# A first norm by plain transposes: raw x^T kept and used again as the residual

## Chip, cores and metric

The kernel runs on one core of a Trainium2 chip. The metric is the device time of one execution in microseconds, median over the runs. PE is the matrix engine, PEld its weight loads, DVE the vector engine, ACT the scalar (activation) engine, POOL the GpSimd engine, SP the engine whose queue issues most transfers.

## The reference, cut to what matters

One layer of a hybrid decoder for 1024 prompt tokens and 8 single-token samples, 1032 tokens in all, model width 1024. What the change touches:

```
def rmsnorm(x, w):
    y = x * rsqrt(mean(x * x, axis=-1, keepdims=True) + EPS)
    return y * w

def decoder_layer(x, ...):
    h = rmsnorm(x, norm1_w)
    q_r, f_r, i_r, g_r, z, xbc_r, dt_r = split(h @ w_in)    # w_in has 6672 columns, the last 16 are dt
    ...                                                     # HGRN2 heads, Mamba-2 mixer
    dt = softplus(dt_r + ssm_dt_bias);  A = -exp(ssm_a_log)
    ...
    x = x + concatenate([o_a, y]) @ w_out                   # the residual
    h = rmsnorm(x, norm2_w)
    ...                                                     # gated MLP with a convolution, second residual
```

All arrays are fp32. A final RMSNorm follows.

## The kernel before

Activations are held transposed: features on the 128 partitions, tokens along the row. The 1032 tokens are cut into three chunks of 344 (`CH`, `chunks`), the model width into eight column tiles of 128 (`KT`). Each fp32 operand of a large product is split in a high part that PE reads at its fast fp32r rate and a low remainder; a product is three matmuls: high times high, low times high, high times low (`prod`, `steps`).

First stage (`first_norm`, L106 to L130, and the loop at L402 to L405). Token tiles of x (128 tokens by 1024, `xt`) are loaded by SP. For three tiles at a time ACT squares them in two halves and sums (L115), DVE and ACT form 1/rms (L116 to L118), and DVE scales an identity by it (`dg`, L119). For each column tile PE multiplies the x tile by `dg` (L127, recorded at L93, the line of the helper `mm`), which transposes and normalises in one step into a PSUM bank (`tp`, four banks). ACT writes the high part `hT_hi` times the norm weight (L128), DVE the low part `hT_lo` (L129). After each group the first two column tiles of the state projection (`first`, tiles 8 and 10, which are B and C of group 0) are multiplied for one chunk of tokens and evicted by `xbc_evict`. A planner orders the instructions of all engines in this stage by its own costs; only PE is written in a fixed order later (`tc.manual_schedule`).

Behind the stage stand the convolution states (`conv_state`, which loads rows `rt` into the shared row buffers of tag "s", eleven of them, and transposes them), the closing of tiles 8 and 10 (`xbc_close`: convolution on DVE, SiLU on ACT), and the dt projection (L426 to L438): its weight is split in high and low halves side by side in 32 columns (`wdt`), and 48 matmuls, 16 a chunk, give `dtr`. Then come the softplus as a chain of short DVE operations (L464 to L480), Exp of `ssm_a_log` (L482), the cumulative sums, and the next column tiles, each with a weight loaded by `wload` (high part cast by ACT at L188, low part by DVE at L189, two buffers each).

The residual is added far later. The output projection runs as jobs `o8.m`, `o12.m`, `o0.m`, `o4.m`. The jobs `o8.m` open the sums: ACT copies the product out of PSUM (L1076), and x is loaded again from its input (`residual_load`, pieces of 128 by 512 with short rows), transposed by PE (L801, L805, tiles `xtp` and `xtd`), and added by DVE (L796). The generator `residual` is spread over the products that follow.

Of the kernel before, what the change touches and what calls it, by code (L numbers as in the profile page):

```python
# [16 lines left out]
P = 128  # L17
# [33 lines left out]
def hybrid_layer(  # L51
# [54 lines left out]
    def first_norm(tiles, then=()):  # L106

        xs = []
        for i in tiles:
            xt, t0, n = xtm[i]  # L110
            sq = half("xn")
            ss = keep.tile([P, 4], F32, tag="ss", bufs=4, name=nm("ss"))
            dg = tl("z", "dg")[:, :P]
            for i in range(2):
                A.activation(sq[:n], xt[:n, i * 512:(i + 1) * 512], AF.Square, accum_out=ss[:n, i:i + 1])  # L115
            V.tensor_tensor(ss[:n, 2:3], ss[:n, 0:1], ss[:n, 1:2], op=ALU.add)  # L116
            A.activation(ss[:n, 3:4], ss[:n, 2:3], AF.Sqrt, bias=epsc[:n], scale=1.0 / DM)
            V.reciprocal(ss[:n, 3:4], ss[:n, 3:4])  # L118
            V.tensor_scalar(dg[:n, :n], ident[:n, :n], ss[:n, 3:4], None, op0=ALU.mult)  # L119
            xs.append((xt, dg, t0, n))  # L120
        for work_ in then:
            work_()
        c0, c1 = xs[0][2], xs[-1][2] + xs[-1][3]
        for k in range(KT):
            tp = bank("tp")
            for xt, dg, t0, n in xs:
                mm(tp[:, t0 - c0:t0 - c0 + n], xt[:n, k * P:(k + 1) * P], dg[:n, :n])  # L127
            A.activation(hT_hi[k][:, c0:c1], tp[:, :c1 - c0], AF.Copy, scale=col("n1", k))  # L128
            V.scalar_tensor_tensor(hT_lo[k][:, c0:c1], tp[:, :c1 - c0], col("n1", k),  # L129
                                   hT_hi[k][:, c0:c1].bitcast(F32), op0=ALU.mult, op1=ALU.subtract)  # L130

# [28 lines left out]
    make_identity(nc, ident)  # L160
    epsc = keep.tile([P, 1], F32, name="epsc")
# [18 lines left out]
    def wload(src, kt, m=P, then=None):  # L180
# [6 lines left out]
        def rounded():  # L187
            A.copy(wh[:, :n], ws[:, :n])  # L188
            V.tensor_tensor(wl[:, :n], ws[:, :n], wh[:, :n].bitcast(F32), op=ALU.subtract)  # L189

        if then is None:
            rounded()
        else:
            then.append(rounded)
# [202 lines left out]
    rounded = []  # L397
    first = [(j, wload(w_in_[0, :, OFF_X + j * P:OFF_X + (j + 1) * P], KT, then=rounded), xbc_open()) for j in (8, 10)]
    for i in range(3, 9):
        load_x(i)  # L400
# [1094 lines left out]
```

## Time and profile before

| | |
|---|---|
| median of 3 runs | 1801.93 us (1798.46 to 1803.37) |
| span of the profiled execution | 1794.6 us (the page gives no other time for it) |
| PE busy | 1741.0 us, 97% |
| DVE, ACT, POOL busy | 1116.6, 789.1, 409.8 us |
| first matmul of the stage, first product | 9.77 us, 15.49 us |
| end of the third chunk's products | 54.33 us |
| end of the dt products | 63.50 us |
| residual transposes | 850 to 939 us |

A row of a timeline reads: start, length, engine, line, operation, output tile and inputs, count in a merged row, and in brackets the idle time before and what ended it. A matmul of two fp32 operands that aren't fp32r is counted as two PE instructions; a transpose as one. Matmuls overlap in the pipeline, so starts, not lengths, give their cost.

### The profile page before, as it was taken

The numbers are of one execution on the slowest core, as the hardware profiler recorded it, in microseconds if no ns is written. First come the engines' busy times: TensorE is split into PE (matmuls) and PEld (weight loads), VectorE is DVE, ScalarE is ACT, GpSimd is POOL, SyncE is SP. The second block draws the span as 40 slices with busy tenths as digits, with TensorE's granted clock in tenths as the row PEclk, the third lists the DMA queues.
The fourth block names the chain that finished last, engine by engine and source line by source line (L and its number), as shares of the span: only waits on it lengthen the run. The fifth ranks groups of instructions, "written<-read, shape, count | busy, mean of one in ns | idle before, by whom it ended". The sixth has DMA issues, their size and how long they took to land.

```text
span 1794.6 us, 38584 instructions
## 1 busy us (share of the span) xinstructions
PE 1741.0 (97%) x16215; PEld 1685.0 (94%) x16215; DVE 1116.6 (62%) x2002; ACT 789.1 (44%) x1414; POOL 409.8 (23%) x415
## 2 busy tenths in 40 slices
PE   7999899999999999999999988999999999999998
PEld 7998798999999999999999978999999999999997
DVE  4658967556555564557746769666666667555545
ACT  6477688454544444345323344333433334111114
POOL 1103331110110110110100364455444542000001
PEclk9999999999999999999999998999999999999999
DMA  5135634553222221235334431222222225422212
GB/s 154 36 98 155 171 100 138 175 147 99 72 77 63 78 79 50 74 96 159 94 107 130 133 116 48 94 73 71 75 85 90 72 71 193 150 95 96 96 60 95
DMA packets 218018, 182.34 MB, mean 102 GB/s; under 512 B 13388, under 2 KB 195158, under 8 KB 217830
## 3 DMA queue, kind: packets, MB, share of 16 engines
q1 hardware_dynamic: 217558, 179.80, 32.5%
q8 instruction: 127, 2.08, 0.5%
q14 instruction: 45, 0.37, 0.1%
q0 software_dynamic: 288, 0.10, 0.0%
HBM read 141.53 MB, written 38.52 MB: 100 GB/s over the span
## 4 chain that ended last, share of the span: by engine, by line
PE 77%; DVE 8%; ACT 6%; DMA 5%; issue 2%; POOL 2%; SPq 0%; DVEq 0%; POOLq 0%; ACTq 0%
PE mm L93 30%; PE ub L93 14%; PE dn L93 13%; PE ua L93 10%; PE a L93 2%; PE o L93 1%; DMA csb<-cs_d 1%; ACT csb L549 1%; PE tp L93 1%; DVE wl L189 1%; DMA Bb<-bc_d 1%; PE kv L93 1%; DMA Sd<-in_state_ssm_dram 1%; DMA out_dram<-Sd 1%; DVE xbc L352 1%
## 5 line engine op out<-in xcount | busy, mean ns | idle before, releaser
L93 PE MATMUL mm<-hh,wh 128*128 128x344 f32 x1248 | 406.2, 326 | 2.6 <-ACT sz L685 2.6
L93 PE MATMUL mm<-hl,wh 128*128 128x344 f32 x1248 | 403.9, 324 | 0.0
L93 PE MATMUL mm<-hh,wl 128*128 128x344 f32 x1248 | 402.8, 323 | 0.0
L93 PEld LDWEIGHTS mm<-hh,wh 128*128 128x128 f32 x1248 | 234.6, 188 | 5.9 <-ACT sz L685 2.9
L93 PEld LDWEIGHTS mm<-hh,wl 128*128 128x128 f32 x1248 | 234.9, 188 | 2.4 <-issue 1.2
L93 PEld LDWEIGHTS mm<-hl,wh 128*128 128x128 f32 x1248 | 234.6, 188 | 2.5 <-issue 0.9
L188 ACT CAST wh<-ws 128x1024 fp32r<-128x1024 f32 x96 | 100.6, 1048 | 265.4 <-PE dn L93 135.8
L93 PE MATMUL ub<-ul,wh 128*128 128x258 f32 x704 | 199.6, 284 | 4.2 <-DVE ul L1182 4.2
L93 PE MATMUL ub<-uh,wh 128*128 128x258 f32 x704 | 201.1, 286 | 2.0 <-ACT uh L1181 2.0
L93 PE MATMUL ub<-uh,wl 128*128 128x258 f32 x704 | 200.8, 285 | 0.0
L93 PE MATMUL dn<-ah,wh 128*128 128x256 f32 (+1 forms) x640 | 180.7, 282 | 1.2 <-DVE x L1425 1.2
L93 PE MATMUL dn<-al,wh 128*128 128x256 f32 (+1 forms) x640 | 180.3, 282 | 0.0
L93 PE MATMUL dn<-ah,wl 128*128 128x256 f32 (+1 forms) x640 | 179.9, 281 | 0.0
L93 PE MATMUL mm<-mh,wh 128*128 128x258 f32 x512 | 148.2, 290 | 10.7 <-DVE x L1078 8.1
L189 DVE TENSOR_TENSOR wl<-ws,wh 128x1024 fp32r<-128x1024 f32 x96 | 125.3, 1306 | 52.5 <-ACT wh L188 52.3
L93 PE MATMUL ua<-ul,wh 128*128 128x258 f32 x528 | 148.9, 282 | 0.9 <-DVE ul L1182 0.9
L93 PE MATMUL ua<-uh,wl 128*128 128x258 f32 x528 | 149.4, 283 | 0.0
L93 PE MATMUL ua<-uh,wh 128*128 128x258 f32 x528 | 149.2, 282 | 0.0
L93 PE MATMUL mm<-ml,wh 128*128 128x258 f32 x512 | 146.5, 286 | 0.0
L93 PE MATMUL mm<-mh,wl 128*128 128x258 f32 x512 | 146.1, 285 | 0.0
L93 PEld LDWEIGHTS ub<-ul,wh 128*128 128x128 f32 x704 | 134.6, 191 | 4.9 <-DVE ul L1182 4.9
L93 PEld LDWEIGHTS ub<-uh,wh 128*128 128x128 f32 x704 | 134.2, 191 | 2.5 <-ACT uh L1181 2.5
(331 smaller groups left out, 3925.0 us busy)
## 6 DMA issues: line engine op xcount, KB each, us to landing
ws<-in_w_in_dram SPq DMA_DIRECT2D x52, 512.0 KB
ws<-in_w_up_dram SPq DMA_DIRECT2D x44, 512.0 KB
ws<-in_w_out_dram SPq DMA_DIRECT2D x24, 512.0 KB
act_d<-val SPq DMA_DIRECT2D x22, 516.0 KB
al<-act_d SPq DMA_DIRECT2D x22, 516.0 KB
ws<-in_w_down_dram SPq DMA_DIRECT2D x22, 512.0 KB
ml<-mix_d SPq DMA_DIRECT2D x48, 172.0 KB
csb<-cs_d SPq DMA_DIRECT2D x32, 256.0 KB
```

The source lines that it names most:

```text
L93: PE.matmul(out, lhsT, rhs, start=start, stop=stop)
L188: A.copy(wh[:, :n], ws[:, :n])
L189: V.tensor_tensor(wl[:, :n], ws[:, :n], wh[:, :n].bitcast(F32), op=ALU.subtract)
L352: V.scalar_tensor_tensor(acc[:, :n], ext[:, q:q + n], col(wname, q * ntile + j), acc[:, :n], op0=ALU.mult, op1=ALU.add)
L549: A.activation(csb3[:, h, :], csb3[:, h, :], AF.Relu, scale=-1.0, bias=cst[:, h0 + h:h0 + h + 1])
```

## The change

- x is transposed by plain PE transposes (`turned`). The raw transposed tile is copied out of PSUM (`copied`: five of eight by ACT, three by DVE) into a row buffer and stored by POOL's queue in a scratch tensor `xT_d`.
- 1/rms is no longer in the transpose: the identity scaled by 1/rms is multiplied by a matrix of ones (`rows`), which puts 1/rms of each token on all partitions. DVE multiplies raw x^T by the norm weight and by it (`normed`), ACT casts the high part, and `low` subtracts (on POOL for column tiles 2 and 5, else on DVE).
- The order on PE, ACT and DVE is written out: transposes run four steps ahead of the products (`LAG`), the next group's squares and statistics and the weights' splits are dealt out over the steps, and the products of the two column tiles and of dt run per column tile, in three PSUM banks. In the first chunk the products with low weights and of dt are held three steps back.
- The dt products leave their place behind the stage. Exp of `ssm_a_log` joins the Exp of the softplus.
- The residual loads `xT_d`, two pieces of 516 tokens a column tile, and POOL adds them; its transposes go.

```
-    def first_norm(tiles, then=()):
-        ...
-        for k in range(KT):
-            tp = bank("tp")
-            for xt, dg, t0, n in xs:
-                mm(tp[:, t0 - c0:t0 - c0 + n], xt[:n, k * P:(k + 1) * P], dg[:n, :n])
-            A.activation(hT_hi[k][:, c0:c1], tp[:, :c1 - c0], AF.Copy, scale=col("n1", k))
-            V.scalar_tensor_tensor(hT_lo[k][:, c0:c1], tp[:, :c1 - c0], col("n1", k),
-                                   hT_hi[k][:, c0:c1].bitcast(F32), op0=ALU.mult, op1=ALU.subtract)
+    xT_d = dram.tile([KT, P, NT], F32, name="xT_d")
...
-    for c in range(NCH):
-        first_norm(range(3 * c, 3 * c + 3), () if c else rounded)
-        for j, w, ext in first:
-            xbc_evict(j, ext, c, chunks[c], prod(w, 0, P, hT_hi, hT_lo, chunks[c]))
+    load_x(3)
+    SP.dma_start(wdt_s, w_in_[0, :, OFF_DT:OFF_DT + 16].rearrange("(k p) m -> p k m", p=P))
+    for i in range(4, 9):
+        load_x(i)
...
+        def stats(self):
+            ss = self.ss
+            V.tensor_tensor(ss[:, 0:3], self.sq[:, 0, 0:3], self.sq[:, 1, 0:3], op=ALU.add)
+            A.activation(ss[:, 0:3], ss[:, 0:3], AF.Sqrt, bias=epsc, scale=1.0 / DM)
+            V.reciprocal(ss[:, 0:3], ss[:, 0:3])
+            self.dg = tl("z", "dg").rearrange("p (a t) -> p a t", t=P)
+            V.tensor_tensor(self.dg, ident.unsqueeze(1).to_broadcast([P, 3, P]),
+                            ss[:, 0:3].unsqueeze(2).to_broadcast([P, 3, P]), op=ALU.mult)
+        def rows(self):
+            self.rb = bank("rb", "nx")
+            for i, (xt, t0, n) in enumerate(self.tiles):
+                mm(self.rb[:, t0 - self.c0:t0 - self.c0 + n], ones[:n], self.dg[:n, i, :n])
...
+    def turned(s):
+        g, k = groups[s // KT], s % KT
+        tps[s] = bank("tp")
+        for xt, t0, n in g.tiles:
+            PE.transpose(tps[s][:, t0 - g.c0:t0 - g.c0 + n], xt[:n, k * P:(k + 1) * P], ident[:n, :n])
+    def low(u):
+        g, k = groups[u // KT], u % KT
+        (G if k in (2, 5) else V).tensor_tensor(hT_lo[k][:, g.cs], hns.pop(u), hT_hi[k][:, g.cs].bitcast(F32), op=ALU.subtract)
+    def copied(u):
+        g, k = groups[u // KT], u % KT
+        raws_x[u] = raw = half("xr")[:, :g.w]
+        if k % 3 == 1:
+            V.tensor_copy(raw, tps.pop(u)[:, :g.w])
+        else:
+            A.copy(raw, tps.pop(u)[:, :g.w])
+        G.dma_start(xT_d[k][:, g.cs], raw)
+    def normed(u):
+        g, k = groups[u // KT], u % KT
+        hn = half("hn")[:, :g.w]
+        V.scalar_tensor_tensor(hn, raws_x.pop(u), col("n1", k), g.rb[:, :g.w], op0=ALU.mult, op1=ALU.mult)
+        A.copy(hT_hi[k][:, g.cs], hn)
+        hns[u] = hn
+        if u:
+            low(u - 1)
...
+    beside = {0: lambda: weight_high(1), 1: lambda: weight_low(0, 0), 2: lambda: weight_low(1, 0),
+              3: dt_weight, 4: lambda: weight_low(0, 1), 5: lambda: weight_low(1, 1)}
...
+    def products(v):
+        c, k = divmod(v, KT)
+        if k == 0:
+            accs[:] = [psmm.tile([P, 512], F32, tag="mm", name=nm("mm"))[:, :CH] for _ in range(2)]
+            accs.append(psmm.tile([P, 512], F32, tag="mm", name=nm("dt"))[:32, :CH])
+        parts = [[(0, 0), (0, 1), (0, 2)], [(1, 0), (1, 1), (1, 2)], [(2, 0), (2, 1)]]
+        if c == 0 and k < KT - 1:
+            now = [(0, 0), (1, 0), (0, 1), (1, 1)]
+            held.append((k, [(0, 2), (1, 2), (2, 0), (2, 1)]))
+            for w in now:
+                first_mm(c, w, k, k == 0 and w[1] == 0, False)
+            if len(held) > 3:
+                kk, ws_ = held.pop(0)
+                for w in ws_:
+                    first_mm(c, w, kk, kk == 0 and w == (2, 0), False)
+            return
+        for i, ws_ in enumerate(parts):
+            for kk, hw in held:
+                for w in hw:
+                    if w[0] == i:
+                        first_mm(c, w, kk, kk == 0 and w == (2, 0), False)
+            for w in ws_:
+                first_mm(c, w, k, k == 0 and w[1] == 0, k == KT - 1 and w == ws_[-1])
+            if k == KT - 1:
+                if i < 2:
+                    xbc_evict(first[i][0], first[i][2], c, chunks[c], accs[i])
+                else:
+                    A.copy(dtr[:32, chunks[c]], accs[2])
+        held.clear()
+    with tc.manual_schedule(engines={mybir.EngineType.PE, mybir.EngineType.Activation, mybir.EngineType.DVE}):
+        groups.append(Group(0))
+        for i in range(3):
+            groups[0].square(i)
+        groups[0].stats()
+        for s in range(NS + LAG):
+            if s < NS:
+                turned(s)
+            if 0 <= s - LAG + 2 < NS:
+                copied(s - LAG + 2)
+            if s == LAG - 1:
+                weight_high(0)
+            u = s - LAG + 1
+            if 0 <= u < NS:
+                c, k = divmod(u, KT)
+                if k == 0:
+                    groups[c].rows()
+                normed(u)
+                if u in beside:
+                    beside[u]()
+                if c + 1 < NCH:
+                    if k == 1:
+                        groups.append(Group(c + 1))
+                    if k in (1, 3, 4):
+                        groups[-1].square((1, 3, 4).index(k))
+                    if k == 5:
+                        groups[-1].stats()
+                if u == NS - 1:
+                    low(u)
+            if s >= LAG:
+                products(s - LAG)
...
-    for c, cs in enumerate(chunks):
-        ps = psmm.tile([P, 512], F32, tag="mm", name=nm("dt"))
-        for k in range(KT):
-            mm(ps[:32, :CH], wdt[:, k, :], hT_hi[k][:, cs], start=(k == 0), stop=False)
-            mm(ps[:32, :CH], wdt[:, k, :], hT_lo[k][:, cs], start=False, stop=(k == KT - 1))
-        A.copy(dtr[:32, cs], ps[:32, :CH])
...
     def residual_load(m):
-        ms = slice(m * P, (m + 1) * P)
-        xs = [tl("d", "xs")[:, :512] for _ in range(2)]
-        xd = small.tile([ND, P], F32, tag="xd", name=nm("xd"))
+        xs = [tl("d", "xs")[:, :2 * QW] for _ in range(2)]
         for i in range(2):
-            fetch(xs[i].rearrange("p (i m) -> p i m", m=P),
-                  x_prompt[0, i * 512:(i + 1) * 512, ms].rearrange("(i p) m -> p i m", p=P))
-        fetch(xd, x_sample[:, 0, ms])
-        return xs, xd
-    def residual(out, xs, xd):
-        def add(x_, ps):
-            V.tensor_tensor(x_, x_, ps, op=ALU.add)
-        for i0 in range(2):
-            ps = bank("xtp")
-            for i in range(4):
-                PE.transpose(ps[:, blk[i]], xs[i0][:, blk[i]], ident)
-            if i0 == 0:
-                add(out[0][:, 0:512], ps)
-                ps = bank("xtd", "nx")
-                PE.transpose(ps[:, :ND], xd, ident[:ND, :ND])
-                add(out[1][:, 508:516], ps[:, :ND])
-            else:
-                add(out[0][:, 512:516], ps[:, 0:4])
-                add(out[1][:, 0:508], ps[:, 4:512])
+            fetch(xs[i], xT_d[m][:, 2 * i * QW:2 * (i + 1) * QW])
+        return xs
+    def residual(out, xs):
+        for o_, x_ in zip(out, xs):
+            G.tensor_tensor(o_, o_, x_, op=ALU.add)
             yield
```

89 lines of the change are left out of this document (52 added, 37 removed).

## The prediction

> **What bounds the kernel now.** I read the page's first table, then busy time by stretch, then the groups of instructions, then the order of time in the two places that the change touches: the first 66 us and the residual around 850 us.
>
> ```profile
> span 1794.6 us, 38584 instructions
> PE 1741.0 (97%) x16215; PEld 1685.0 (94%) x16215; DVE 1116.6 (62%) x2002; ACT 789.1 (44%) x1414; POOL 409.8 (23%) x415
> ```
>
> PE is busy for 97% of the span. Time is won by taking work from PE, or by starting it earlier, where PE is the bound. The busy time by stretch (start:end, length, each engine's busy time and count, granted clock, DMA share, GB/s) tells where that is:
>
> ```profile
> core 0: us, PE busy (x) PEld busy (x) DVE busy (x) ACT busy (x) POOL busy (x), PEclk, DMA share, GB/s
> 0.00:9.77 9.77, 0.24 (x1) 0.18 (x2) 1.44 (x9) 5.67 (x15) 8.40 (x26) 1.00 0.85 265
> 15.49:25.86 10.37, 10.37 (x76) 10.37 (x75) 5.51 (x19) 9.63 (x30) 0.00 (x0) 1.00 0.30 70
> 54.33:63.50 9.17, 9.17 (x65) 6.30 (x65) 6.27 (x14) 4.51 (x7) 0.34 (x2) 1.00 0.40 111
> 840.00:945.00 105.00, 104.74 (x1227) 100.83 (x1228) 65.36 (x138) 37.82 (x81) 11.39 (x7) 0.98 0.37 113
> ```
>
> PE stands still until 9.77, is full where the first products run, and is busy for 104.74 of 105 us around the residual. But ACT is nearly full as well (9.63 of 10.37) in the first chunk: a lighter PE would uncover ACT there. The page gives the span, 1794.6; the median of the runs is 1801.9, 7.3 above. I sum against the span and carry the 7.3 over.
>
> **First stage, what PE sheds.** The order of time on PE, then the chain, then the dt products alone by stretch:
>
> ```profile
> 12.62 3.12 PE L93 MATMUL tp<-dg,xt 128*128 128x128 f32 x14 [0.34 <-DVE dg L119]
> 15.49 0.56 PE L93 MATMUL mm<-hh,wh 128*128 128x344 f32 x2
> 25.86 4.85 PE L93 MATMUL tp<-dg,xt 128*128 128x128 f32 x42
> 46.52 7.81 PE mm L93 x48
> 54.33:63.50 9.17, 8.32 (x48) 4.96 (x48) 0.00 (x0) 0.86 (x2) 1.00 0.40 111
> sum 44.56, PE 22.17 PEld 20.29 DVE 13.51 ACT 12.77; mean PE 4.43 PEld 4.06 DVE 2.70 ACT 2.55
> ```
>
> A product of 344 columns costs 7.81/48 = 0.163 us. The diagonal products (each counted as two instructions) cost 4.85/42 = 0.115 us an instruction late and 0.22 early; all 144 took 22.17 us (last row, the tile tp from 9.77 to 54.33). The first product starts at 15.49; the dt products end at 63.50.
>
> What a plain transpose costs, the residual's rows show, in order of time:
>
> ```profile
> 850.09 0.60 PE L801 MATMUL xtp<-ident,xs 128*128 128x128 f32 x4
> 850.62 0.22 PE L805 MATMUL xtd<-ident,xd 8*128 8x8 f32 x1
> 850.78 0.38 PE L93 MATMUL mm<-mh,wh 128*128 128x258 f32 x1
> 851.00 0.28 PE L93 MATMUL mm<-ml,wh 128*128 128x258 f32 x1
> 851.11 0.28 PE L93 MATMUL mm<-mh,wl 128*128 128x258 f32 x1
> 851.83 0.60 PE L801 MATMUL xtp<-ident,xs 128*128 128x128 f32 x4
> 852.19 0.37 PE L93 MATMUL mm<-mh,wl 128*128 128x258 f32 x1
> 852.39 0.28 PE L93 MATMUL mm<-mh,wh 128*128 128x258 f32 x1
> ```
>
> Four transposes hold PE from 851.83 to 852.19, 0.09 each, and the next product is 0.08 late (852.39 - 852.19 against 0.11 to 0.12). So a step of three costs 0.27 + 0.08 = 0.35. The ones products for 1/rms are nine, 18 instructions of 0.115, 2.1 us. The dt products keep their number, 48, and only move into the chunks; what they do today is to cover the weights of the next column tile.
>
> **First stage, when products can start.** ACT and DVE rows, groups by form (count | busy, mean ns | idle before):
>
> ```profile
> 7.43 0.63 ACT L115 ACTIVATE xn<-xt 128x512 f32<-128x512 f32 x1 [0.34 <-DMA xt<-in_x_prompt_dram]
> 8.76 0.19 ACT L115 ACTIVATION_READ_ACCUMULATOR xn<-xt 128x1 f32 x1
> L115 ACT ACTIVATE xn<-xt 128x512 f32<-128x512 f32 x16 | 10.0, 625 | 2.7 <-DMA xt<-in_x_prompt_dram 2.7
> L115 ACT ACTIVATION_READ_ACCUMULATOR xn<-xt 128x1 f32 x16 | 3.1, 192 | 0.0
> L117 ACT ACTIVATE ss<-ss,epsc 128x1 f32<-128x1 f32 x8 | 2.3, 288 | 0.7 <-DVE ss L116 0.7
> L129 DVE SCALAR_TENSOR_TENSOR hl<-tp,vcol,hh 128x384 fp32r<-128x384 f32 x16 | 9.6, 614 | 2.5 <-ACT hh L128 2.3
> L188 ACT CAST wh<-ws 128x1024 fp32r<-128x1024 f32 x4 | 4.2, 1047 | 7.0 <-PE mm L93 5.8 <-DMA ws<-in_w_in_dram 1.2
> L362 ACT COPY ext<-mm 128x344 f32<-128x344 f32 x4 | 1.8, 440 | 5.8 <-PE mm L93 5.8
> L1017 ACT CAST mh<-ml 128x344 fp32r<-128x344 f32 x48 | 21.4, 481 | 7.6 <-DMA ml<-mix_d 6.5 <-PE mm L93 0.7
> ```
>
> The third x tile is squared at 8.95. Then follow two short sums and a reciprocal on DVE with the square root between (0.3 for the root, an estimate of 0.3 for the DVE pair), the scaled identity of 384 columns (0.61 from the row of that width), six cold PE instructions of 0.22 (1.3), the multiplication from PSUM (0.61) and the cast of the high half (0.5): 8.95 + 3.7 = 12.65; with a few hops, 13.0. Four transposed tiles lie ready by then, made while PE waits today. The start gains 2.5 us on 15.49.
>
> Then ACT sets the pace in chunk 0. In its written order it still has: the second weight 1.05, five copies of raw x^T at about 0.5 (between the 0.44 and 0.61 rows), seven high casts at 0.5, six squares with their reads at 0.82 for the next group (4.9), the dt weight and the root 0.6: 12.5 us, to 25.5. After the last cast come the low part (0.6) and the products held back for the last step, 20 x 0.163 = 3.3: chunk 0 ends at 29.4. From there PE bounds again: 128 products x 0.163 = 20.9, 12 steps of transposes x 0.35 = 4.2, one set of ones products 0.7, together 25.8; plus 1.8 for waits in chunk 1, where ACT waits behind its in-order evictions and three high casts then come just in time: 57.0. The state transposes and the vector columns that lie among today's dt products follow, 9.17 - 48 x 0.163 = 1.3 us: 58.3. And the cover is gone: the next weight's cast and subtraction (1.05 + about 1.2) can only start when the last chunk has released its buffer, so 1.0 of it, an estimate, shows on PE. 59.3 against 63.5: **-4.2 us**. Bounds: no ACT wait at all, 13.0 + 192 x 0.163 + 20 x 0.35 + 1.4 + 1.3 = 54.0, gives -9.5; the upper bound is 0, when new waits eat all of it.
>
> **SP's queue.** The order of time on it:
>
> ```profile
> 9.31 0.38 SPq L103 DMA_DIRECT2D xt<-in_x_sample_dram  x1
> 9.86 0.40 SPq L428 DMA_DIRECT2D wdt_s<-in_w_in_dram  x1
> 18.82 9.45 SPq L178 DMA_DIRECT2D rt<-in_state_conv_ssm_dram  x3
> ```
>
> The dt weight goes ahead of x tiles 4 to 8, one issue of 0.4 later for each; tile 4 is squared only near 19 in my walk: 0. The three loads of convolution states take buffers from the pool that raw x^T and its products now rotate through, so they come near the stage's end. If they are late, PE can take the next column tile first, which costs 0 unless its weight is the thing missing, and that 1.0 is in the sum.
>
> **Residual.** Removed from PE, per column tile: 850.09 to 851.00 less a spacing of 0.12, and 851.83 to 852.39 less 0.12, so 0.79 + 0.44 = 1.23 us; eight of them, **-9.8 us**, on an engine that is 99.8% busy there. Nothing else is late next: DVE is 62% busy and sheds 24 additions, ACT is 36% busy. The additions go to POOL, 11% busy, 16 of them; the sum is only read again an output-weight pair later. The loads are as many bytes from a scratch tensor. Bounds: -9.8, and 0 if the POOL additions come late.
>
> **POOL and its queue.** POOL gets 24 stores of x^T, six of the low parts, and the additions. The same tile operation took 1.04 and 3.23 us, and a POOL load this long from issue to landing (last number):
>
> ```profile
> 124.76 1.04 POOL L563 TENSOR_TENSOR xde<-xdt,dec 128x512 f32<-128x512 f32 x1 [1.92 <-DVE xdt L562]
> 153.31 3.23 POOL L563 TENSOR_TENSOR xde<-xdt,dec 128x512 f32<-128x512 f32 x1 [1.08 <-DVE xdt L562]
> vrows<-in_ffn_conv_w_dram POOLq DMA_DIRECT2D x1, 33.0 KB, 5.1
> ```
>
> In chunk 0 a low part at 3.2 hides under ACT; in chunk 1 two of them are within the 1.8 above. [...]
>
> Moving the Exp of a_log and the ones memset changes ACT and POOL alone, off the path: 0.
>
> Sum: -4.2 - 9.8 = -14.0 on the span, 1780.6; beside the median, **1788**.
>
> **Rivals.**
> - *First stage bound by PE alone* (PE runs ahead of ACT by the held products and four PSUM banks): -9.5 - 9.8, 1783. Against it is the ACT share of 9.63 in 10.37.
> - *First stage gives nothing*, ACT's evictions and the uncovered weight eat it; residual alone, 1792.
> - *Cold PE.* Early spacing is twice the late one (0.22, 0.115). If chunk 0's 64 products run at twice 0.163, PE needs 10.4 us more, of which PE's idle time before 29.4 takes 2.4: +8, 1796. [...]
> - *Slower: the raw-x^T buffers.* They come from 11 shared buffers, each step takes some 2.4, so a buffer must be back after 4.6 steps. It is held for copy 0.5, issue 0.5 and the landing L. A step is then at least (1.0 + L)/4.6, against 14.0/8 = 1.75 of PE work. With L = 5.1 that is 1.3, hidden; the whole gain is gone when 24 steps grow by 0.58 each, at L = 9.7. At L = 11 it is +20.6 - 14.0, 1808.5. Against it: 5.1 was measured with the DMA queues 85% busy; but these stores have 176 KB.
> - *The residual does not pay*: the POOL additions arrive late, 1798. Against: 11.39 of 105 us POOL.
>
> **How the numbers follow.** Chances: my forecast 0.50 (its own range 1782 to 1794), PE alone 0.14, nothing in the first stage 0.16, cold PE 0.07, buffers 0.06, residual lost 0.07. 0.3% is 5.4 us, about what a measurement of this kernel tells from none: faster means under 1796.5. Forecast, PE alone and stage-nothing are faster, nearly all of 0.80, and half of cold PE: 0.82; same takes the other half, the lost residual and the tails, 0.12; slower 0.06. The range 1777 to 1800 leaves out the buffers and the tail of PE alone.
>
> **What would show it.** In the profile after: first product at about 13; PE idle in short waits on ACT or DVE until about 29; the dt eviction at about 57, against 63.5; no PE rows for xtp; POOL additions near 850 with no PE wait on them; PE's busy sum lower by about 20. Wrong if copies of raw x^T wait on DMA, or if products wait on POOL's low parts in most steps, or if the products of the first chunk lie 0.3 us apart.

## The result: 14 us slower, not 14 us faster

The changed kernel takes 1815.41 us (median of 4 runs, 1812.56 to 1818.12) beside 1801.93; the ratio is 1.008, interval 1.0063 to 1.0097. I had said 1788. Its profiled execution took 1816.4 with a span of 1814.3. Later runs of the kernel before gave medians of 1799.2 to 1801.3; each ratio below is against the runs beside it. The profile of the kernel before caught an execution on the short side of its runs: its span lies 19.7 below that of after where the medians differ by 13.5, so some 6 us of a difference that is read late in the two traces can be chance. TensorE is the rows' PE, VectorE their DVE, ScalarE their ACT and GpSimd their POOL; *before* and *after* are the kernel before and the changed kernel.

The page after:

```profile
span 1814.3 us, 38399 instructions
PE 1739.3 (96%) x16089; PEld 1679.9 (93%) x16089; DVE 1121.9 (62%) x1985; ACT 787.9 (43%) x1418; POOL 452.3 (25%) x461
```

The transposes are gone and yet PE's busy sum fell by 1.7 us, not 20. The mean granted clock fell from 0.992 to 0.985: of 1814.3 us that is 27 us' worth of clock not granted, against 14 before. PE waited more, and behind several of its waits it ran at half rate (granted clock 0.50 from 26.1 to 32.9). Such a time at half of the granted clock is called a *window* below; its place is that of the clock's record in the trace (the expectations put it about 1.2 us earlier). The stretches of the kernel after that answer to those shown of before (granted clock, DMA share and GB/s last):

```profile
0.00:9.77 9.77, 3.00 (x13) 2.46 (x13) 1.06 (x7) 5.90 (x15) 6.73 (x20) 1.00 0.86 264
13.93:29.36 15.43, 7.88 (x35) 6.32 (x35) 7.82 (x16) 8.95 (x23) 4.46 (x8) 0.89 0.54 194
861.80:966.80 105.00, 101.49 (x1192) 99.12 (x1193) 62.60 (x112) 38.81 (x84) 33.53 (x23) 0.95 0.37 115
```

PE starts its products at 13.93 (forecast: 13.0), and is then busy half of the time. PE's own order of time (start, length, in brackets the idle time before and its releaser) shows one great hole:

```profile
15.32 0.78 PE L93 MATMUL mm<-hl,wh 128*128 128x344 f32 x2
19.84 0.58 PE L93 MATMUL mm<-hl,wh 128*128 128x344 f32 x2 [0.74 <-POOL hl L428]
29.36 0.94 PE L93 MATMUL mm<-hl,wh 128*128 128x344 f32 x2 [6.51 <-DVE hl L428]
```

and the chain of work back from there what filled it (start, length):

```profile
15.49 12.63 DMA xT_d<-xr
28.22 0.61 DVE hn L442
```

A store of raw x^T issued at 15.49 landed 12.63 us later; VectorE's next product needed its buffer and began at 28.22; TensorE got its low part at 29.36. This is the rival of the buffers, to which I gave 6 in 100. The store was not the only late one: the five issued from 15.49 to 23.06 landed after a median of 11.4 us, but only the first had a waiter. The busy times by 2 us show why they were late:

```profile
20.00:22.00 2.00, 2.00 (x13) 1.67 (x14) 1.54 (x3) 1.96 (x7) 0.57 (x1) 1.00 0.05 0
22.00:24.00 2.00, 0.84 (x7) 0.54 (x5) 0.00 (x0) 0.76 (x3) 0.55 (x1) 1.00 0.10 21
26.00:28.00 2.00, 0.00 (x0) 0.00 (x0) 0.00 (x0) 0.00 (x0) 0.00 (x0) 0.52 0.74 286
```

A DMA share of 0.05 at 0 GB/s is the time of about one of sixteen engines, busy with next to no bytes. What SP had issued is in its order of time:

```profile
13.47 1.81 SPq L569 DMA_DIRECT2D d_bc<-in_ssm_d_dram  x2
```

These are the two loads of d_bc, which spread 16 numbers over 128 rows with a stride: 1024 elements of four bytes. In the two us from 20 the trace has 216 packets, all under 512 bytes, so some 110 per us; that they are those of d_bc, a_rowd below confirms. The kernel before has the same quiet time (share 0.05 from 18 to 22, 0.04 to 24); its SP row of rt, 9.45 us for three loads, was caught in it, and nobody waited:

```profile
20.00:22.00 2.00, 2.00 (x14) 2.00 (x14) 1.67 (x6) 1.26 (x4) 0.00 (x0) 1.00 0.05 0
```

The stage's end (the last dt product in after) and the first bg product, which comes once tiles 8 and 10 are closed, stand in the rows of the tiles dt and bg (shortest, median and longest in ns, then first and last start). Before:

```profile
L93 PE MATMUL dt<-hl,wdt x24: 313/320/373, 54.8 to 63.2; 128*32 128x344 f32 x24
L93 PE MATMUL bg<-xbc,xbc x32: 273/275/276, 121.9 to 315.0; 128*128 128x128 f32 x32
```

and after:

```profile
L93 PE MATMUL dt<-hl,wdt x24: 313/321/488, 21.9 to 71.1; 128*32 128x344 f32 x24
L93 PE MATMUL bg<-xbc,xbc x32: 272/275/275, 139.5 to 333.8; 128*128 128x128 f32 x32
```

The last dt product starts 7.9 us late, and the *stretch* from there to the first bg product grows from 58.7 to 68.4: two losses of about the same size. Behind the first bg product the two traces differ by 2.1 us only (1674.8 against 1672.7), where the residual should have won 9.8. Within the stretch the waits (us in total, times, longest) and the busy times of after show a wait for ScalarE's eviction ext of the next column tile and a window behind it, from 90.9 to 97.8, most of which the second row holds:

```profile
PE mm L93 <- ACT ext L336: 4.0, 1, 4.0
```

```profile
89.80:96.60 6.80, 4.92 (x17) 4.93 (x18) 6.36 (x20) 3.65 (x7) 0.56 (x5) 0.58 0.01 2
```

### The profile page after: what moved, and what is told of

It is laid out like the page before. It is cut to its first block, busy times and chain, and to the rows that moved or that the text cites. A ratio compares the mean times of both kernels' runs of the same rounds, so it can differ in the third digit from the quotient of the medians.

```text
span 1814.3 us, 38399 instructions
## 1 busy us (share of the span) xinstructions
PE 1739.3 (96%) x16089; PEld 1679.9 (93%) x16089; DVE 1121.9 (62%) x1985; ACT 787.9 (43%) x1418; POOL 452.3 (25%) x461
## 4 chain that ended last, share of the span: by engine, by line
PE 76%; DVE 9%; DMA 5%; ACT 4%; issue 3%; POOL 2%; SPq 0%; DVEq 0%; POOLq 0%; ACTq 0%
PE mm L93 31%; PE ub L93 14%; PE dn L93 13%; PE ua L93 10%; PE a L93 2%; PE o L93 1%; DVE xbc L326 1%; DMA csb<-cs_d 1%; ACT csb L664 1%; PE kv L93 1%; DVE wl L166 1%; DMA out_dram<-Sd 1%; DMA xT_d<-xr 1%; DMA Bb<-bc_d 1%; POOL Cb L767 1%
## 5 line engine op out<-in xcount | busy, mean ns | idle before, releaser
L93 PE MATMUL mm<-hh,wh 128*128 128x344 f32 x1248 | 412.1, 331 | 7.3 <-ACT ext L336 4.0
```

The source lines that it names most:

```text
L93: PE.matmul(out, lhsT, rhs, start=start, stop=stop)
```

## Experiments

**The slow packets.** *a_rowd* (on the changed kernel), *b_rowd* (the same edit on the kernel before) and *a_spstore* (the changed kernel with the last edit alone), code shortened:

```
+    d_row = const.tile([P, 16], F32, name="d_row")
+    SP.dma_start(d_row, ssm_d.to_broadcast([P, 16]))
     for h2 in range(2):
-        SP.dma_start(d_bc[64 rows], <16 numbers, strided> .to_broadcast([64, 8]))
+        V.tensor_copy(d_bc[rows, :], d_row[rows].rearrange("p (j h) -> p h j", h=2)[:, h2, :])
# a_spstore alone:
-        G.dma_start(xT_d[k][:, g.cs], raw)
+        SP.dma_start(xT_d[k][:, g.cs], raw)
```

> The changed kernel with one edit: ssm_d is loaded as one row for all partitions (64-byte pieces) and spread by two small DVE copies, where before two loads took it in 4-byte pieces. Theory A: those 1024 four-byte packets keep one DMA engine busy from about 17 to 27 us, the store of raw x^T issued at 15.5 shares that engine and lands at 28.1, and DVE waits 6.7 us for its buffer. Then the longest store takes under 6 us, DVE no longer waits for a store, the half clock at 25 to 32 us is gone, and the time falls by 6 to 10 us, to 1805 to 1809. Rival B: stores from POOL's queue are slow while the inputs load, whatever else is queued: the longest store stays over 9 us and the time within 3 us of 1815.

Measured: 1809.12, ratio 1.0056 (1.0041 to 1.0071), 6.3 under after by the medians and 4.3 by the ratios, whose intervals overlap; so the size rests on the traces too. Theory A holds, its time just missed: the longest store took 5.8, VectorE's wait for it and the window behind it are gone. The stores' landing and the rows of dt and bg in a_rowd:

```profile
DMA to landing us min/median/max: 2.0/2.4/5.8
```

```profile
L93 PE MATMUL dt<-hl,wdt x24: 317/320/426, 23.6 to 65.3; 128*32 128x344 f32 x24
L93 PE MATMUL bg<-xbc,xbc x32: 273/275/275, 133.8 to 327.0; 128*128 128x128 f32 x32
```

The stage is 5.8 us shorter; the stretch is 68.5 (68.4 in after).

> The kernel before with ssm_d loaded as one row of 16 and put in place by two copies on VectorE. The slow packets lie between 17 and 27 us there too, but the trace of the kernel before shows only SP's load of rt caught in them, for which nobody waits. Theory A (the slow packets cost only where something waits for a transfer behind them): 1800 to 1802.5, no difference from the kernel before, though rt's load is no longer 8.6 us long. Rival (the loads of x and of the first weights are held by them too): 1 to 4 us faster, with the first products earlier than now.

Measured: 1799.50, 0.9997 (0.9984 to 1.001). SP's row of rt took 1.17 us instead of 9.45, and the time is the same. Nobody waited behind the slow packets here, and they cost nothing.

> The kernel after with the stores of raw x^T issued by SP instead of GpSimd. Theory A (the store that landed after 12.6 us stood behind the four-byte packets of ssm_d's loads on one DMA engine): whoever issues it, a store of that time takes 8 us or more, or SP, which has ssm_d's loads ahead of it, issues it later; the first stage ends at 69 us or later and the time is 1811 to 1818. Rival (GpSimd's way of issuing is slow): no store takes over 4 us, the dt products end at 66 or before, and the time is 1806 to 1810.

Measured: 1806.58 (one run), dt's end at 62.8. The time is the rival's, the mechanism is not: the quiet time is still there (share 0.05), only from 22 to 30, because SP now issued five stores ahead of d_bc's loads. I had assumed the other order. A store behind the loads is late here too, but VectorE waits only 2.1 us for it (until 32.60) instead of 6.7. That GpSimd's queue is not slow in itself, a_rowd's stores through it show (median 2.4 us to landing, longest 5.8). SP's order of time and a busy time of a_spstore:

```profile
11.79 6.79 SPq L437 DMA_DIRECT2D xT_d<-xr  x5
19.61 1.41 SPq L569 DMA_DIRECT2D d_bc<-in_ssm_d_dram  x2
```

```profile
24.00:26.00 2.00, 1.56 (x11) 1.21 (x9) 2.00 (x4) 0.02 (x1) 0.54 (x1) 1.00 0.05 0
```

**The closing of tiles 8 and 10.** *a_lowf* (on the changed kernel, as all runs named a_) gives lowf a buffer that is not ext's:

```
-    lowf = tl("e", "lowf")[:, :4 * P].rearrange(...)
+    lowf = half("lowf").rearrange(...)
```

> The changed kernel with one edit: the tile lowf (POOL's masks, 3.6 us) no longer takes one of the two buffers of the convolution inputs, but a row buffer. Theory A: behind the first stage the next column tile's first eviction waits for such a buffer behind the convolution of tile 10 and lowf, PE stands 4.0 us at 87.7 and then runs 6.8 us at half clock, because the dt products no longer stand there to cover it. Then PE's wait for ext falls under 1 us, the half clock at 90 to 97 us is gone, and the time falls by 5 to 8 us, to 1807 to 1810. Rival B: the convolutions on DVE alone hold the buffer that long: the wait only gets smaller by 1 to 2 us and the time stays at 1812 or more.

Measured: 1814.53, 1.0087 (1.0070 to 1.0103). The wait for ext is 2.9 instead of 4.0, the time the same: rival B. *a_rowd_cov* is a_rowd with the dt products back behind the stage:

```
-        parts = [[(0, 0), (0, 1), (0, 2)], [(1, 0), (1, 1), (1, 2)], [(2, 0), (2, 1)]]
+        parts = [[(0, 0), (0, 1), (0, 2)], [(1, 0), (1, 1), (1, 2)]]
     BT[0], CT[0] = (xbc_close(j, ext) for j, w, ext in first)
+    for c, cs in enumerate(chunks): ...        # the dt loop of the kernel before
```

> The kernel after with ssm_d loaded as one row (as in a_rowd) and, beside that, the dt products taken out of the first stage and put back behind the closing of tiles 8 and 10, as in the kernel before; dt's weight is still rounded within the stage. Theory C (the lost cover): in the kernel before the 48 dt products ran while VectorE and ScalarE closed tiles 8 and 10, and from their end to the first bg product it took 58.7 us; with the dt products inside the stage that stretch is 68.5 us in a_rowd, with a TensorE wait for ext and a half-clock window at 84 in it. Put back, the stretch is 58.5 to 61 again, no half-clock window lies between 80 and 100, the dt products end at 65 to 67, the first bg product comes at 124 to 127 instead of 133.8, and the time is 1799 to 1803. Rival D (the stretch is long because the convolutions of tiles 8 and 10 and the Exp in front of the eviction hold VectorE and ScalarE whatever TensorE does): TensorE waits for ext as before, only later or shorter; bg comes at 131 or later, and the time is 1806 to 1810.

Measured: 1808.24, 1.0034 (1.0018 to 1.005). Both theories are half right. The stretch is 58.8, TensorE doesn't wait for ext, no window lies there. But the stage's 144 products of tiles 8 and 10 end at 65.0, as late as with the 48 dt products among them: taking these out did not shorten the stage. What was won behind the stage was lost in it, with a window of 10.2 us from 46.5 (rows of dt and bg, and a busy time, of a_rowd_cov):

```profile
L93 PE MATMUL dt<-hl,wdt x24: 315/320/368, 65.4 to 73.8; 128*32 128x344 f32 x24
L93 PE MATMUL bg<-xbc,xbc x32: 273/275/275, 132.6 to 327.5; 128*128 128x128 f32 x32
```

```profile
45.20:55.40 10.20, 8.96 (x32) 7.02 (x31) 4.25 (x11) 3.60 (x10) 2.18 (x4) 0.56 0.13 46
```

*b_dt_in* is the converse: the kernel before, with the dt products of each chunk right behind its products of tiles 8 and 10:

```
     for c in range(NCH):
         first_norm(...); products and evictions of tiles 8 and 10
+        the 16 dt products of chunk c, and A.copy(dtr[:32, chunks[c]], ps[:32, :CH])
```

> The kernel before, with its first norm and its residual as they were, and one edit: dt's weight is loaded and rounded at the start, and the 16 dt products of each column chunk stand right behind that chunk's products of tiles 8 and 10, in the first stage, as in the kernel after. Theory C (the lost cover): the dt products end at 61.5 to 64.5 as before, but nothing lies beside the closing of tiles 8 and 10: TensorE waits 2.5 us or more for ext, a half-clock window follows it between 75 and 95, the stretch from the last dt product to the first bg product grows from 58.7 to 65 to 69 us, and the time is 1807 to 1812. Rival D (the dt products cost the same at either place): the stretch stays under 62 us, and the time is 1800 to 1803.5.

Measured: 1801.74, 1.0012 (0.9999 to 1.0024). The stretch is nearly theory C's, the time is rival D's: the stretch grows by 6.1 to 64.8, with a wait for ext and a window at 79.5, but the dt products end 2.2 earlier. The cover that I priced at 1.0 is worth some 6 us in the stretch, but moving the products costs 1.4 us in the whole, 4.3 by the upper end of the interval. It is not the main loss. Rows of dt and bg, and the wait, in b_dt_in:

```profile
L93 PE MATMUL dt<-hl,wdt x24: 317/319/322, 25.7 to 61.0; 128*32 128x344 f32 x24
L93 PE MATMUL bg<-xbc,xbc x32: 273/275/275, 125.8 to 317.9; 128*128 128x128 f32 x32
```

```profile
PE mm L93 <- ACT ext L362: 2.5, 1, 2.5
```

*a_rowd_early* brings the closing forward (code shortened):

```
+    rts = [tl("d", "rt")[:24, :512] for _ in range(3)]      # loaded behind the x tiles
+    closing = {24: [state_cols(0), state_cols(1)], 25: [state_cols(2), vec_cols(1, "mx")], 26: [vec_cols(2, "mx")]}
             if s >= LAG:          # in step s, ahead of the products
                 products(s - LAG)
```

> a_rowd (the kernel after with ssm_d loaded as a row) with the transposes of the convolution's old rows and of the other two blocks of columns (cst and vps) done ahead of the last four steps of the first stage, from other buffers and PSUM banks, so that the convolutions of tiles 8 and 10 can begin when their products end; the dt products stay in the stage. Theory C in its narrow form (what lay under the dt products was above all this 5 us chain of transposes and copies): the first convolution on ScalarE begins within 3 us of the last eviction, TensorE's wait for ext falls from about 4 to under 1.5 us and the half-clock window at 84 goes, the stretch from the last dt product to the first bg falls from 68.5 to 61 to 64.5 us, and the time is 1802 to 1805.5. Rival (VectorE's convolutions and ScalarE's Silu and Exp in front of ext's eviction hold it, whenever they begin): the wait stays 2.5 us or more with a half-clock window behind it, the stretch is 66 us or more, 1806.5 to 1811.

Measured: 1815.13, 1.0084 (1.0064 to 1.0104). Both theories fall: it is slower, and for another reason. TensorE's wait in the stretch is for the next tile's weight; VectorE made its low part behind 7.46 us of convolutions that now came first, and the clock's record shows a window from 72.5 to 86.1. The wait and VectorE's order of time in a_rowd_early:

```profile
PE mm L93 <- DVE wl L166: 6.8, 1, 6.8
```

```profile
71.36 7.46 DVE L326 SCALAR_TENSOR_TENSOR xbc<-ext,vcol,xbc 128x1056 f32<-128x1056 f32 x6
78.95 2.35 DVE L166 TENSOR_TENSOR wl<-ws,wh 128x1024 fp32r<-128x1024 f32 x2
```

The weights have two buffers, and the changed kernel interleaves tiles 8 and 10 step by step, so both come free only at the stage's last products. The kernel before did tile 8 ahead of 10 within a chunk. *a_early_seq* does that in the last four steps (tile 8, then 10, then dt):

```
+        if c == NCH - 1 and KT - 4 <= k < KT - 1:
+            for w in parts[0]:
+                first_mm(c, w, k, False, False)
+            held.append((k, parts[1] + parts[2]))
+            return
```

> a_rowd_early with the last four steps of the stage in another order: tile 8's products for all four, then tile 10's, then dt's, so that tile 8's weight buffers come free some 3 us before the stage ends, as in the kernel before, and the next tile's weight can be rounded ahead of the convolutions. Theory G (a_rowd_early lost because the next weight, free only with the last product, was rounded behind 7.5 us of convolutions): TensorE's wait of 6.8 us for wl and the half-clock window of 13.7 us at 71 go, the first bg product comes at 126 to 129.5 (140.6 in a_rowd_early, 133.8 in a_rowd), the time is 1800 to 1804.5. Rival (closing the two tiles cannot go faster: ext's eviction or a weight holds TensorE again): bg at 132 or later, 1806.5 to 1812.

Measured: 1803.89, 1.0024 (1.0009 to 1.0038), 11 us under a_rowd_early by an order of the same products. The theory holds in each of its numbers; nothing in the stretch keeps TensorE waiting. Its length, 57.7, can't be set beside the kernel before's 58.7, as the transposes of the closing now lie ahead of the last dt product and that product is last by order; the first bg product can: at 129.1 it comes 4.7 before a_rowd's and 7.2 behind the kernel before's. What is left is a late stage, with a window at 26.1 that a_rowd does not have.

```profile
L93 PE MATMUL dt<-hl,wdt x24: 316/320/488, 22.2 to 71.4; 128*32 128x344 f32 x24
L93 PE MATMUL bg<-xbc,xbc x32: 273/275/275, 129.1 to 322.9; 128*128 128x128 f32 x32
```

**Inside the stage.** *a_rowd_vlow* and *a_rowd_warm*, both from a_rowd:

```
-        (G if k in (2, 5) else V).tensor_tensor(hT_lo[k][:, g.cs], ...)       # a_rowd_vlow
+        V.tensor_tensor(hT_lo[k][:, g.cs], ...)
+    def idle_mm(n):                                                          # a_rowd_warm
+        for _ in range(n):
+            mm(groups[0].rb[:, 384:512], ident, ident)
+    idle_mm(4); groups[0].rows(); idle_mm(4)
```

> a_rowd with the low parts of the blocks that GpSimd made (two of eight in each chunk, 1.0 us each there) made by VectorE like the others. Theory H (GpSimd's low parts are late and TensorE waits for them, 1.5 and 1.0 us in a_rowd): the dt products end 1.5 to 3 us earlier (62.3 to 63.8 instead of 65.3) and the time is 1806 to 1808. Rival (VectorE, 80 per cent busy in the first chunk, is as late with six more of 0.57 us): dt products end at 64.5 to 66.5, 1808.5 to 1810.5.

Measured: 1807.97, 1.0054 (1.0034 to 1.0074); dt's end at 65.2. The stage is the rival's: waits for GpSimd's low parts (3.2 us in a_rowd) became waits for VectorE's, 5.2 instead of 1.5 us. The median lies in theory H's range, but the ratio can't be told from a_rowd's 1.0056.

> a_rowd with eight products of 128x128 that nothing uses, put where TensorE idles before the first real products (four ahead of the row of 1/rms, four behind it), into columns of that bank that are otherwise unused. Theory I (the first chunk's products run 0.285 us apart until 24.0 instead of 0.158 because TensorE had idled before them; in the kernel before it was busy without a gap from 9.8 to 15.2 and its products were 0.158 apart from the first): they are 0.158 apart from about 15 on, the dt products end at 62.5 to 64 and the time is 1805.5 to 1808. Rival (the first chunk is paced by ScalarE and VectorE, so that faster products only wait): dt products end at 64.5 or later and the time is 1808 to 1810.5.

Measured: 1805.35, 1.0034 (1.0022 to 1.0045). Two of the first pairs of products on PE in a_rowd:

```profile
15.51 0.78 PE L93 MATMUL mm<-hl,wh 128*128 128x344 f32 x2
17.30 0.78 PE L93 MATMUL mm<-hl,wh 128*128 128x344 f32 x2
```

and in a_rowd_warm:

```profile
17.21 0.48 PE L93 MATMUL mm<-hl,wh 128*128 128x344 f32 x2
21.88 0.59 PE L93 MATMUL mm<-hl,wh 128*128 128x344 f32 x2 [1.41 <-POOL hl L433]
```

The products are fast from the first, as the theory has it, but the stage is not: they wait for GpSimd (4.7 us for 3.2) and ScalarE instead and dt ends at 66.7, as the rival has it. The time is the theory's, or a little less. Its span is 3.7 us shorter, all of it won after the first bg product, where the run had fewer half-clock windows; that the eight products caused this is not shown, and the interval overlaps a_rowd's.

**The residual.** *a_oldres* takes the stores away and restores the old residual; *b_newres* puts the new residual alone into the kernel before; *b_newres_v* is the same with the additions on VectorE. These two leave out the transposed copy of x: they add rows of x_prompt as they lie, so their output is not the layer's, and they price the new residual without what its x^T costs. The code is shortened; in b_newres the minus line is the changed kernel's.

```
-        G.dma_start(xT_d[k][:, g.cs], raw)                                   # a_oldres, and the old residual
-            fetch(xs[i], xT_d[m][:, 2 * i * QW:2 * (i + 1) * QW])              # b_newres: the new residual,
+            fetch(xs[i], x_prompt[0, m * P:(m + 1) * P, 508 * i:508 * i + 2 * QW])   # from rows of x_prompt
-            G.tensor_tensor(o_, o_, x_, op=ALU.add)                            # b_newres_v
+            V.tensor_tensor(o_, o_, x_, op=ALU.add)
```

> The changed first stage without the stores of raw x^T, and the residual as before the change (x loaded again, transposed on PE, added by DVE). Theory A: no buffer waits for a store, so the stage ends 6 to 8 us earlier than in the changed kernel (dt products done by 66 instead of 71), while the residual costs PE its 10 us again: 1813 to 1819. Rival B: the written order is what makes the stage long, stores or not: the dt products still end after 69 and the time is 1821 or more.

Measured: 1812.40, 1.0070 (1.0055 to 1.0085), dt's end at 62.6: without stores there is no late buffer, as theory A has it, but the stretch is 68.5 still, and the residual's gain is missing. The stage ends 2.7 us before a_rowd's too, and a_spstore's 2.5 before: the two runs in which no store goes through GpSimd. In a_rowd GpSimd's second low part stands behind a store for whose raw copy GpSimd waited 1.50 us; it starts at 26.64, where it starts at 23.43 in a_oldres and 23.54 in a_spstore, and TensorE waits for it (a_rowd):

```profile
27.71 0.59 PE L93 MATMUL mm<-hl,wh 128*128 128x344 f32 x2 [1.49 <-POOL hl L428]
```

That this order on GpSimd is what is left of the stage's loss is not shown: a_rowd_vlow, without these low parts, ended no earlier, the full clock also came earlier in the two (17.9 and 20.3, 23.8 in a_rowd), and no run joins a_rowd's load with stores by SP.

> The kernel before with the residual's cost of the changed kernel alone: pieces of the same size are loaded from x in rows (not transposed, so what is added is other data than the residual) and added by POOL; no transposes on PE. Theory A: PE sheds 9.8 us around 850 us and keeps 7 to 10 of them: 1792 to 1795. Rival B: POOL's additions come late or PE's next wait at the norm takes them back: 1798 or more.

Measured: 1796.28, 0.9973 (0.9959 to 0.9986), 4.9 under the kernel before, between the two theories.

> b_newres (the kernel before with the new residual alone, its operand read straight from rows of x_prompt, so other data is added) with the sixteen additions on VectorE instead of GpSimd. Theory E (the additions on GpSimd slow VectorE beside them, and TensorE then waits for q): the groups ml, k and tt of VectorE go back to their durations of before (544, 866 and 313 ns instead of 660, 1038 and 501), TensorE's wait of 3.5 us for q goes, and the gain against the kernel before is 8 to 10 us (1791 to 1793). Rival F (VectorE has the additions to do itself, as it had before: its wait for q stays or is as long, and only the transposes' 8.7 us less are won, with the clock giving some back): 1795 to 1798, the same as b_newres.

Measured: 1793.77, 0.9955 (0.9939 to 0.997), 7.2 under it, again between the two theories; the intervals of b_newres and b_newres_v overlap. VectorE's k group (count | busy, mean ns | idle before) is back at its old length of 866 ns, tt only in part (313 ns before, 501 in b_newres, 411 here); in b_newres:

```profile
L858 DVE TENSOR_TENSOR k<-k,tt 128x512 f32<-128x512 f32 x6 | 6.2, 1038 | 5.2 <-PE a L93 5.2
```

and in b_newres_v:

```profile
L858 DVE TENSOR_TENSOR k<-k,tt 128x512 f32<-128x512 f32 x6 | 5.2, 862 | 2.5 <-PE a L93 2.5
```

but TensorE's wait for q stayed (3.5 in b_newres, here in b_newres_v), so the additions on GpSimd did not make it:

```profile
PE a L93 <- DVE q L859: 3.3, 1, 3.3
```

Where half of the gain is missing, the busy times show: from the first mm<-mh product to the last of dms, and on to the first n2ms, in the kernel before:

```profile
840.00:888.60 48.60, 48.55 (x771) 45.78 (x772) 36.97 (x78) 19.32 (x45) 8.54 (x5) 0.96 0.42 126
888.60:1008.90 120.30, 120.07 (x990) 118.72 (x989) 64.12 (x130) 41.65 (x76) 14.03 (x16) 1.00 0.40 124
```

and in b_newres_v:

```profile
841.90:890.10 48.20, 44.89 (x735) 42.97 (x736) 37.23 (x70) 19.51 (x45) 9.09 (x5) 0.93 0.41 127
890.10:1005.20 115.10, 114.89 (x954) 114.50 (x953) 63.71 (x122) 41.53 (x76) 14.13 (x16) 1.00 0.42 129
```

Half of the 64 transposes lay in each part. In the second, the time falls by 5.2 us, four times 1.23 and a little. In the first, PE is busy 3.7 us less and takes nearly the same time (48.2 for 48.6): there PE's products a need VectorE's q, and without the transposes PE waits 3.3 us for it; the granted clock is lower too (0.93 for 0.96, one window more).

**Together.** *a_best* is a_rowd_early with a_lowf's edit and the additions on VectorE; *a_best3* is a_early_seq with the eight products and the additions on VectorE; *a_best4* is a_best3 with the products of x^T's low parts one step behind the others:

```
+            for kk, w in behind:                   # hl of the step before
+                first_mm(c, w, kk, False, False)
+            behind[:] = [(k, (0, 1)), (k, (1, 1))]
-            now = [(0, 0), (1, 0), (0, 1), (1, 1)]
+            now = [(0, 0), (1, 0)]
```

> a_rowd_early with two more edits: lowf in one of the shared buffers (as in a_lowf), so that GpSimd can clear ext earlier, and the residual additions on VectorE. If the parts add up (a_rowd 1809.1, early 5 to 6.5 less, lowf 0 to 1 less, additions 0 to 3 less): 1799 to 1803, about the kernel before. Rival (early gives nothing): 1805 to 1809.

Measured: 1812.92, 1.0074 (1.0056 to 1.0092): above the rival's range. The early closing gains nothing here either: TensorE waits 6.5 us for the next weight's low part.

> a_early_seq with the eight unused products of a_rowd_warm ahead of the first chunk and the residual additions on VectorE. If the parts add up (a_early_seq 1803.9; the window of 6.8 us at 24.9 goes, 3.4 us; the additions 0 to 3 us): 1797 to 1801, not to be told from the kernel before or a little faster. Rival (the half-clock windows come elsewhere instead): 1801 to 1805.

Measured: 1796.53, 0.9968 (0.9953 to 0.9984), a little under the expected range.

> a_best3 with the products of the low parts of x^T one step behind those of the high parts, so that TensorE has a step's work before it needs the low part that VectorE or GpSimd makes last. Theory J (TensorE's waits for hl, 5 to 7 us in the stage, make its end late): the waits for hl fall under 2 us, the dt products end 3 to 5 us earlier than in a_best3, and the time is 2 to 5 us lower, 1793 to 1798. Rival (ScalarE, VectorE and GpSimd pace the stage together; the wait moves to hh): the dt products end within 1.5 us of a_best3's and the time is the same within 2 us.

Measured: 1795.85, 0.9965 (0.995 to 0.998). Its dt products end at 70.5 and a_best3's at 69.7; the waits for hl fell from 5.2 to 4.4 and those for hh rose from 1.5 to 2.7: the rival holds. Both kernels beat the kernel before by about 0.3%, 19 us under the changed one. They don't win it in the first stage: their first bg product comes at 127.4 and 128.2, 5.5 and 6.3 behind the kernel before's 121.9. The new norm still costs; what it gives is the stored x^T, and the new residual that needs it wins more (7.2 in b_newres_v) than the norm loses.

## Why the prediction was wrong, step by step

The sum had two terms, and both failed. The first stage with its closing, -4.2, came out as 17.6 late at the first bg product (139.5 against 121.9): 7.9 in the stage and 9.7 behind it. The residual, -9.8, gave half to three quarters of that.

- *When products can start*: 13.93 for 13.0. Right within a microsecond.
- *ACT sets the pace in chunk 0, to 29.4*: wrong, this step failed first. TensorE stood 6.5 us for a buffer, and chunk 0's products ended near 35 even in a_rowd, which has no late store: the first product came 1.1 late there (14.1), three waits for low parts (two of them for GpSimd's, which stand behind its stores and had no price in the sum) and one for a weight took 3.1, and the products ran 0.285 apart until 23.8.
- *L = 5.1 for the landing of a store*: this term of the buffers' rival was mis-sized; the forecast itself put it at nothing. I took L from a load when the queues were busy with large packets; the store landed after 12.63 with 1024 packets of four bytes ahead of it, and the wait went with them (a_rowd). The rival's formula was not tested: it takes a late landing for all 24 stores, and here five were late and the loss was one stop of 6.5. The row that told it was in the prediction, rt's 9.45 us for three loads (1.17 in b_rowd); I read it as a matter of SP's queue.
- *A transpose step of 0.35*: the steps that waited for nothing in the last chunk took 1.82 us (a_rowd, 53.15 to 54.98) instead of 1.65. Over sixteen steps that is 2.7.
- *The cold-PE rival*: its mark was there (products 0.285 apart in chunk 0; the clock's record first shows the full clock at 19.2, and the 1.00 that the views give ahead of it is no entry), and its price was not: a_rowd_warm took the mark away and the stage ended no earlier. What made the full clock come late is not shown, since the eight products also filled gaps.
- *The cover of the dt products, priced at 1.0*: 6.1 in the stretch (b_dt_in), most of it not seen in the whole time there (1.4). In after, TensorE's wait in the stretch is for ext (4.0); the next weight, on which the 1.0 was put, held TensorE only when the convolutions came early, because interleaving frees both of its buffers at once: a_early_seq against a_rowd_early shows that this order alone is worth 11 us then.
- *SP's queue, 0*: no run shows a cost of its order by itself; what two of its loads consist of was the cost.
- *Residual, -9.8*: -4.9 (b_newres) to -7.2 (b_newres_v). "99.8% busy there" was a mean over 105 us: it hid a part where the transposes themselves were the filling. That additions on GpSimd make VectorE's products beside them longer shows in the durations (k 1038 ns for 862); its price is 2.3 us by the medians of the two runs, whose intervals overlap.
- *PE's busy sum lower by 20*: 1.7 lower. Work at half clock is longer (products 0.287 apart for 0.158, in after), and the sum had no term for it; how much of the missing 18 us that is, no run shows, since of the 27 us of clock not granted (14 before) a part lies over idle time.
- Left open: between the last bg and the last ms product, after took 95.8 us where the kernel before took 90.8, and the other kernels with the new norm between 89.8 (a_lowf) and 94.3. In after TensorE waits 3.2 us there for VectorE's vd (0.7 before) and the clock's record shows a window of 6.8 us; no run isolates its cause. Part of it is chance: from the first bg product to the end, a_rowd took 1673.2 and a_rowd_warm, with the same instructions there, 1668.1.

## What to carry to other kernels

A transfer of a few kilobytes in pieces of four bytes took some ten microseconds here (1024 packets at about 110 per us): harmless until the first large transfer with a waiter lands behind it, so look for times with a tiny DMA share at no bytes (0.05 at 0 GB/s here) before putting stores into a ring of buffers. Work that a change takes from the busiest engine is only worth time where that engine had no gap that the work was filling; ask it for each place, not for a mean over them. When products of two tiles are interleaved, both weight buffers are freed last: the order of release decides when the next tile's weights can be rounded. And a gain can lie under a loss: here the residual's 5 to 7 us lay under 17.6 us lost ahead of it, and only runs of each part alone showed both.

## What the runs showed of the hardware

- In these traces the granted clock fell to half in pieces of 3.41 us and multiples (3.41 us at 237.7, 6.83 at 90.9 and 10.24 at 1101.3 in after, 13.7 at 72.5 in a_rowd_early), in the first 100 us behind waits of TensorE: one of 4.0 us (after), or several of 0.5 to 1.0 (a_rowd_cov, ahead of 46.5). In the 3.4 us ahead of a fall TensorE was busy for 0.14 us (after, ahead of 26.1), 1.32 (a_early_seq, ahead of 26.1) and 2.36 (a_rowd_cov, ahead of 46.5; 2.37 from 36.3 to 39.7 brought no fall there). Products lay 0.287 apart in a window and 0.158 outside (after, 91.7 to 99), so by these two spacings a window cost nearly half its length where TensorE had work.
- A granted clock of 1.00 at the kernel's start said nothing here: the clock's record in a trace has its first entry, full clock, at 15.4 us in before, 13.8 in a_rowd_warm, 19.2 in after and 23.8 in a_rowd, and the views give 1.00 for the time ahead of it. In a_rowd products ran 0.287 apart up to 23.8 and 0.155 behind it; the spacing of equal products was the safer sign.
- Packets of four bytes went at about 110 per us (216 in the two us from 20, at a DMA share of 0.05, after), and a store of 192 KB behind them took 12.6 us where the median was 2.5 (after). One load in pieces of 64 bytes took the place of the two in a_rowd, and the longest store took 5.8.
